# Attention: a unit's transposes directly ahead of the next unit's scores, its value products one turn later

## The chip, the cores and the metric

One core of a Trainium2 chip runs the whole program. The metric is device time in microseconds, the median of repeated executions. TensorE is called PE in what follows, VectorE is DVE, ScalarE is ACT, GpSimd is POOL and SyncE, which issues most loads, is SP.

## What is computed

A diffusion backbone of four layers, over 256 latent tokens (a grid of 4 rows by 64 columns) and 256 context tokens of width 1024. Layers 0 and 3 mix tokens by attention, layer 1 by a convolution module, layer 2 by a gated convolution; after each comes an MLP with squared ReLU. The change touches the two attention layers alone:

```python
q, k, v = split_heads(h_lat @ wqkv, 3)          # 16 heads of 64
q = q * ATTN_SCALE
...
s_lat = jnp.einsum("bhqd,bhaqkd->bhqak", q_r, k_nb)   # window of 16 columns in every grid row
s_lat = s_lat + bias_r
s_ctx = jnp.einsum("bhqd,bhcd->bhqc", q_r, k_c)       # all context keys
p = jax.nn.softmax(concatenate([s_lat, s_ctx]), axis=-1)
...
o = p_lat @ v_nb + p_ctx @ v_c
...
o_lat = o_grid.reshape(b, l, d) @ wo
```

In layer 0 the context tokens are queries too, with a softmax over context keys; in layer 3 only latent tokens are.

## The kernel before

**Units.** Heads are taken in pairs, eight of them. A pair has three units in layer 0 (latent tokens 0 to 127, latent tokens 128 to 255, all context tokens) and the first two of them in layer 3, so there are 24 units and 16. A unit is worked in these steps:

- scores (`attn_scores`, line 714): for both heads a product of 512 columns in three terms, since queries and keys are kept as a high and a low part. One PSUM tile for each head; the pool `mm` has six.
- softmax (`softmax`, lines 729 to 739), for one head after the other: DVE adds bias and mask (729) and takes the negated row maximum (734), ACT takes the exponential (736) with the row sum, DVE its reciprocal (737) and the scaling (739).
- transposes (`attn_transpose`, line 748): PE turns the four blocks of the first head and then of the second through two PSUM tiles of the pool `x`, and ACT copies each tile out (749).
- value products (`attn_out`, line 758): both heads' matmuls alternate. After a pair's last unit `finish` (772, 773) splits the output into high and low part.

**What stands between the steps.** `attn_pairs` is a generator. It yields at fixed places, and `attention` advances it from inside another stream of matmuls: first the query and key projections of the coming pairs (`qks`, one step is six matmuls), later the first half of the output projection (`first_half`, one step is twelve). `interleave` gives six turns of the generator to eight steps of the stream in layer 0 and four to eight in layer 3; beside `first_half` it gives twelve or ten turns to seven steps, so there the pieces stand closer. PE's order is exactly the order in which the code is written here (`manual_schedule`, lines 879 to 896). The other engines' orders come from a scheduler that places their instructions when it builds the program; each engine then works its own list in that order.

**What else is in those lists.** DVE and ACT also split the next pair's weights into high and low part (`split`, lines 223 and 224, two tiles of 128x1024 for each pair), evacuate the projections (820 to 825), update the residual stream (591), and DVE accumulates modulation vectors in the background (lines 314 and 318) from rows that SP loads (line 310). These rows' buffers (tag `mraw`, four of them) are shared with the bias tiles `e` of the softmax: a row is loaded into a buffer once line 729 has read the bias tile there. In layer 0 the background also runs on PE (lines 373 and 382). The transposed probabilities `pt` and the split weights share the tag `w` with ten buffers.

```python
for i in range(len(items) + 1):
    if i < len(items):
        ...
        soft[i] = self.attn_scores(q[hp], k[hp], u, bias[hp])
    yield
    if i > 0:
        ...
            self.attn_transpose(x, u, pt[:, hh])
    yield
    if i > 0:
        weigh(*items[i - 1], pt)
```

Of the kernel before, what the change touches and what calls it, by code (L numbers as in the profile page):

```python
# [8 lines left out]
F32 = mybir.dt.float32  # L9
# [7 lines left out]
P = 128  # L17
D = 1024
KT = D // P
LAT = 256  # L20
# [13 lines left out]
class Net:  # L34
# [726 lines left out]
    def attn_pairs(self, slot, hps, q, k, v, o, units):  # L761

        nc = self.nc
        items = [(hp, u) for hp in hps for u in units]
        bias, soft, pts, out = {}, {}, {}, {}

        def finish(hp):
            ps = out.pop(hp)
            hi, lo = self.hid(F32R), self.hid(F32R)
            n = NTOK if len(units) > 2 else LAT  # L770
            src, a, b = self.turned(ps[:, :n]), self.rows64(hi[:, :n]), self.rows64(lo[:, :n])
            nc.scalar.activation(out=a, in_=src, func=AF.Copy)
            nc.vector.tensor_tensor(out=b, in0=src, in1=a.bitcast(F32), op=ALU.subtract)
            o[hp] = (hi, lo)

        def weigh(hp, u, pt):
            if u == 0:
                out[hp] = self.ps()
            self.attn_out(out[hp], pt, v, hp, u)
            if u == units[-1]:  # L780
                finish(hp)

        for i in range(len(items) + 1):
            if i < len(items):
                hp, u = items[i]
                for p in (hp, hp + 1):
                    if p in hps and p not in bias:
                        bias[p] = [self.bias_tile(slot, 2 * p + hh, q[hp][0] if slot == 0 and hp == 0 else None)
                                   for hh in range(2)]
                soft[i] = self.attn_scores(q[hp], k[hp], u, bias[hp])  # L790
            yield
            if i > 0:
                hp, u = items[i - 1]
                pt = self.wtile([2, 4, P] if u < 2 else [2, 2, LAT], F32)
                for hh, x in enumerate(soft.pop(i - 1)):
                    self.attn_transpose(x, u, pt[:, hh])
            yield
            if i > 0:
                weigh(*items[i - 1], pt)

    def value(self, v, acts, g, tt, i, part, ps):


        if tt not in ps:
            ps[tt] = self.ps()
        s = slice(tt * P, (tt + 1) * P)
        self.mm3(ps[tt], (acts[i][0][:, s], acts[i][1][:, s]), part, i == 0, i == KT - 1)
        if i == KT - 1:
            v[tt, g] = self.work.tile([P, 512], F32, tag=f"u{4 * g + tt}", name=self.name("v"))
            self.nc.scalar.copy(out=v[tt, g], in_=ps[tt])  # L810
# [565 lines left out]
```

## Time and profile before

| what | value |
|---|---|
| median of 3 runs (lowest, highest) | 2176.44 us (2175.43, 2177.57) |
| the profiled execution, its span | 2173.36 us, 2171.5 us |
| PE busy over the span | 2132.5 us (98%) |
| DVE, ACT busy | 1537.9 us (71%), 829.9 us (38%) |
| stretch of attention turns in layer 0 | 104 to 283 us of the span |
| stretch of attention turns in layer 3 | 1844 to 1962 us of the span |

PE is busy nearly throughout, so what counts is where it stands still, and in what these two stretches differ from the rest. A matmul's row in the timeline is longer than its share of the engine, since matmuls overlap: the time that a piece of work takes is read from the start of its first row to the start of the next piece.

### The profile page before, as it was taken

Reading aid. Unit: us, or ns where it says so; the run is one execution under the profiler, and the core shown is the slowest. Engines: PE = TensorE matmul, PEld = TensorE weight load, DVE = VectorE, ACT = ScalarE, POOL = GpSimd, SP = SyncE. Lnnn points to the kernel's source line nnn. Section 1 sums busy time; section 2 is a strip of 40 time slices with the busy share of each in tenths; the row PEclk is TensorE's granted clock in tenths of the full one; section 3 lists DMA queues with packets and bytes.
Section 4 is the critical chain, followed back from the end, with each engine's and each line's share of the span. In section 5 each row is a group of like instructions: output and inputs, shape, how many; then the busy total and the mean of one; then the engine's idle time right before and its main releaser. Section 6 shows DMA issues by size and latency. Waiting matters only on the chain.

```text
span 2171.5 us, 33261 instructions
## 1 busy us (share of the span) xinstructions
PE 2132.5 (98%) x12948; PEld 1782.6 (82%) x12948; DVE 1537.9 (71%) x2727; ACT 829.9 (38%) x1397; POOL 98.5 (5%) x168
## 2 busy tenths in 40 slices
PE   8999999999999999999999999999999999989998
PEld 5777778888889779888888888898888888879998
DVE  5266668986889947978676876597755674778655
ACT  4255534223234226523223332252322333546444
POOL 1122100000000000000000000000000001220000
PEclk9999999999999999999999999999999999999999
DMA  9655544654553551454444444245544535664563
GB/s 302 159 106 118 136 153 153 190 155 154 153 175 112 157 162 50 136 181 152 128 149 148 138 134 145 79 137 175 165 146 140 170 117 131 101 108 155 186 193 107
DMA packets 202188, 318.09 MB, mean 146 GB/s; under 512 B 14669, under 2 KB 67857, under 8 KB 202032
## 3 DMA queue, kind: packets, MB, share of 16 engines
q1 hardware_dynamic: 198080, 309.26, 45.5%
q0 software_dynamic: 3648, 6.61, 4.6%
q8 instruction: 101, 1.65, 0.3%
q14 instruction: 55, 0.45, 0.1%
q10 hardware_dynamic: 304, 0.12, 0.0%
HBM read 313.15 MB, written 2.78 MB: 145 GB/s over the span
## 4 chain that ended last, share of the span: by engine, by line
PE 88%; DVE 4%; ACT 1%; DMA 1%; issue 1%; DVEq 0%; ACTq 0%; SPq 0%
PE mm L106 27%; PE mm L107 26%; PE mm L108 26%; PE mm L1010 2%; PE mm L758 2%; PE mm L714 1%; PE x L748 1%; DVE h L970 1%; DMA mraw<-in_mod_w_dram 1%; DVE w L224 1%; PE mm L373 1%; PE x L492 0%; ACT w L749 0%; PE x L529 0%; DVE t L546 0%
## 5 line engine op out<-in xcount | busy, mean ns | idle before, releaser
L223 ACT ACTIVATE w<-raw 128x1024 fp32r<-128x1024 f32 (+1 forms) x377 | 392.8, 1056 | 683.7 <-PE mm L107 614.3
L106 PE MATMUL mm<-a,w 128*128 128x512 f32 (+2 forms) x1792 | 632.4, 354 | 5.1 <-ACT a L559 4.7
L224 DVE TENSOR_TENSOR w<-raw,w 128x1024 fp32r<-128x1024 f32 (+1 forms) x377 | 452.4, 1219 | 260.8 <-ACT w L223 259.9
L108 PE MATMUL mm<-a,w 128*128 128x512 f32 (+2 forms) x1792 | 624.8, 350 | 4.7 <-DVE w L224 4.7
L107 PE MATMUL mm<-a,w 128*128 128x512 f32 (+2 forms) x1792 | 628.1, 351 | 0.1
L107 PE MATMUL mm<-h,w 128*128 128x256 f32 (+1 forms) x1504 | 505.6, 336 | 0.0
L106 PE MATMUL mm<-h,w 128*128 128x512 f32 (+1 forms) x1376 | 472.2, 344 | 0.0
L108 PE MATMUL mm<-h,w 128*128 128x512 f32 (+1 forms) x1376 | 469.1, 341 | 0.0
L106 PEld LDWEIGHTS mm<-a,w 128*128 128x128 f32 x1792 | 338.6, 189 | 64.0 <-issue 10.2
L108 PEld LDWEIGHTS mm<-a,w 128*128 128x128 f32 x1792 | 339.3, 190 | 52.4 <-DVE w L224 5.9
L107 PEld LDWEIGHTS mm<-a,w 128*128 128x128 f32 x1792 | 339.6, 190 | 45.8 <-DVE a L560 0.8
L318 DVE SCALAR_TENSOR_TENSOR macc<-mraw,cw,macc 128x512 f32<-128x512 f32 x448 | 311.9, 744 | 27.0 <-DMA mraw<-in_mod_w_dram 26.0
L107 PEld LDWEIGHTS mm<-h,w 128*128 128x128 f32 x1504 | 282.8, 188 | 32.0
L106 PEld LDWEIGHTS mm<-h,w 128*128 128x128 f32 x1376 | 258.8, 188 | 37.3 <-issue 2.7
L108 PEld LDWEIGHTS mm<-h,w 128*128 128x128 f32 x1376 | 258.5, 188 | 32.6 <-DVE w L224 0.2
L591 DVE SCALAR_TENSOR_TENSOR x<-mm,mod,x 128x256 f32<-128x256 f32 x288 | 127.5, 477 | 79.5 <-PE mm L108 78.3
L223 ACT ACTIVATE h<-t 128x512 fp32r<-128x512 f32 (+1 forms) x148 | 80.7, 547 | 104.4 <-DVE t L622 90.9
L224 DVE TENSOR_TENSOR h<-t,h 128x512 fp32r<-128x512 f32 (+1 forms) x148 | 86.0, 582 | 25.7 <-ACT h L223 25.4
L622 DVE SCALAR_TENSOR_TENSOR t<-mm,t 128x512 f32<-128x512 f32 (+1 forms) x136 | 78.6, 584 | 35.3 <-ACT t L621 34.8
L621 ACT ACTIVATE t<-mm 128x512 f32<-128x512 f32 (+1 forms) x136 | 69.0, 510 | 89.6 <-PE mm L108 88.7
L736 ACT ACTIVATE t<-mm,s 128x512 f32<-128x512 f32 (+1 forms) x96 | 59.3, 620 | 91.1 <-DVE s L734 83.2
L559 ACT ACTIVATE a<-t,mod 128x256 fp32r<-128x256 f32 x120 | 53.1, 500 | 63.3 <-DVE t L546 63.3
(177 smaller groups left out, 1666.3 us busy)
## 6 DMA issues: line engine op xcount, KB each, us to landing
raw<-in_mlp_w_dram SPq DMA_DIRECT2D x256, 512.0 KB, 4.4
mraw<-in_mod_w_dram SPq DMA_DIRECT2D x288, 256.0 KB, 3.0
raw<-in_na_wqkv_dram SPq DMA_DIRECT2D x64, 256.0 KB, 5.3
raw<-in_mod_w_dram SPq DMA_DIRECT2D x32, 512.0 KB, 4.7
raw<-in_sc_win_dram SPq DMA_DIRECT2D x24, 512.0 KB, 4.4
h<-in_mod_w_dram SPq DMA_DIRECT2D x32, 256.0 KB, 6.5
raw<-in_na_wqkv_dram SPq DMA_DIRECT2D x16, 512.0 KB, 4.7
raw<-in_na_wo_dram SPq DMA_DIRECT2D x16, 512.0 KB, 8.2
```

The costliest lines, as they stand in the source:

```text
L106: mm(out=out, lhsT=a[0], rhs=b[0], start=start, stop=False)
L107: mm(out=out, lhsT=a[0], rhs=b[1], start=False, stop=False)
L108: mm(out=out, lhsT=a[1], rhs=b[0], start=False, stop=stop)
L223: self.nc.scalar.activation(out=hi, in_=src, func=AF.Copy)
L224: self.nc.vector.tensor_tensor(out=lo, in0=src, in1=hi.bitcast(F32), op=ALU.subtract)
L318: nc.vector.scalar_tensor_tensor(out=acc[s], in0=raw, scalar=c, in1=acc[s], op0=ALU.mult, op1=ALU.add)
L559: self.nc.scalar.activation(out=hi[:, c], in_=t, func=AF.Identity, bias=sh)
L591: self.nc.vector.scalar_tensor_tensor(out=x, in0=src[:, o:o + LAT], scalar=self.mod1(layer, m, s, j), in1=x, op0=ALU.mult, op1=ALU.add)
L621: nc.scalar.activation(out=r, in_=src, func=AF.Relu)
L622: nc.vector.scalar_tensor_tensor(out=h, in0=src, scalar=0.0, in1=r, op0=ALU.max, op1=ALU.mult)
L736: nc.scalar.activation(out=soft[:, g], in_=s[:, g], func=AF.Exp, bias=nm[:, i:i + 1], accum_out=sm[:, i:i + 1])
L758: nc.tensor.matmul(out=out[64 * hh:64 * hh + 64, c], lhsT=v[t0 + i, hp // 4][:, f:f + 64], rhs=pt[:, hh, i], start=i == 0, stop=i == n - 1 ...
```

## The change

The loop of `attn_pairs` has two yields a round as before, at other places. Before, a round began with the scores of unit i, and the transposes of unit i-1 came a turn later, its value products another turn later, ahead of the next scores. Now a round begins with the transposes of unit i-1, directly followed by the scores of unit i, and the value products of unit i-1 come one turn later. No instruction is added to PE or taken away.

```diff
--- before.py
+++ after.py
@@ -762,7 +762,7 @@
 
         nc = self.nc
         items = [(hp, u) for hp in hps for u in units]
-        bias, soft, pts, out = {}, {}, {}, {}
+        bias, soft, out = {}, [], {}
 
         def finish(hp):
             ps = out.pop(hp)
@@ -781,22 +781,22 @@
                 finish(hp)
 
         for i in range(len(items) + 1):
+            if i > 0:
+                hp, u = items[i - 1]
+                pt = self.wtile([2, 4, P] if u < 2 else [2, 2, LAT], F32)
+                for hh, x in enumerate(soft.pop()):
+                    self.attn_transpose(x, u, pt[:, hh])
             if i < len(items):
                 hp, u = items[i]
                 for p in (hp, hp + 1):
                     if p in hps and p not in bias:
                         bias[p] = [self.bias_tile(slot, 2 * p + hh, q[hp][0] if slot == 0 and hp == 0 else None)
                                    for hh in range(2)]
-                soft[i] = self.attn_scores(q[hp], k[hp], u, bias[hp])
-            yield
-            if i > 0:
-                hp, u = items[i - 1]
-                pt = self.wtile([2, 4, P] if u < 2 else [2, 2, LAT], F32)
-                for hh, x in enumerate(soft.pop(i - 1)):
-                    self.attn_transpose(x, u, pt[:, hh])
+                soft.append(self.attn_scores(q[hp], k[hp], u, bias[hp]))
             yield
             if i > 0:
                 weigh(*items[i - 1], pt)
+            yield
 
     def value(self, v, acts, g, tt, i, part, ps):
```

On PE, in layer 3 beside the output projection, before: value products (`w_17992` holds turned probabilities), scores of a unit into `mm_18047` and `mm_18048`, and behind them the transposes of the unit before (`t_17963` and `t_17972` are its probabilities).

```order
L758 MATMUL mm_17937<-w_17992,v_16742 64x128 x2
L758 MATMUL mm_17937<-w_17992,v_16747 64x128 x2
L758 MATMUL mm_17937<-w_17992,v_16804 64x128 x2
L758 MATMUL mm_17937<-w_17992,v_16809 64x128 x2
L714 MATMUL mm_18047<-h_17643,h_17544 128x512
L714 MATMUL mm_18048<-h_17643,h_17544 128x512
L714 MATMUL mm_18047<-h_17643,h_17545 128x512
L714 MATMUL mm_18048<-h_17643,h_17545 128x512
L714 MATMUL mm_18047<-h_17644,h_17544 128x512
L714 MATMUL mm_18048<-h_17644,h_17544 128x512
L748 MATMUL x_18074<-ident,t_17963 128x128 x4
L748 MATMUL x_18080<-ident,t_17972 128x128 x4
```

The same place now:

```order
L748 MATMUL x_18048<-ident,t_17976 128x128 x4
L748 MATMUL x_18054<-ident,t_17985 128x128 x4
L714 MATMUL mm_18060<-h_17655,h_17553 128x512
L714 MATMUL mm_18061<-h_17655,h_17553 128x512
L714 MATMUL mm_18060<-h_17655,h_17554 128x512
L714 MATMUL mm_18061<-h_17655,h_17554 128x512
L714 MATMUL mm_18060<-h_17656,h_17553 128x512
L714 MATMUL mm_18061<-h_17656,h_17553 128x512
L758 MATMUL mm_18086<-w_18047,v_16742 64x128 x2
L758 MATMUL mm_18086<-w_18047,v_16747 64x128 x2
L758 MATMUL mm_18086<-w_18047,v_16804 64x128 x2
L758 MATMUL mm_18086<-w_18047,v_16809 64x128 x2
```

The transposes moved ahead of the scores, and the value products of the same unit moved behind them. From a unit's scores to its own transposes there were three turns; now there are two.

On DVE, in layer 3, the softmax of a pair's second unit, before (`mm_` are the scores of the two heads, `macc` the background sum, `mraw` its loaded rows, `w_` and `raw_` the weights that are split):

```order
L729 TENSOR_TENSOR mm_17672<-mm_17672,e_17389 128x256
L729 TENSOR_TENSOR mm_17673<-mm_17673,e_17393 128x256
L734 TENSOR_REDUCE s_17682<-mm_17672 128x1
L737 RECIPROCAL s_17684<-s_17683 128x1
L734 TENSOR_REDUCE s_17691<-mm_17673 128x1
L318 SCALAR_TENSOR_TENSOR macc_17461<-mraw_17647,cw,macc_17461 128x512
L739 TENSOR_SCALAR t_17681<-t_17681,s_17684 128x512
L318 SCALAR_TENSOR_TENSOR macc_17461<-mraw_17650,cw,macc_17461 128x512
L737 RECIPROCAL s_17693<-s_17692 128x1
L821 SCALAR_TENSOR_TENSOR h_17730<-mm_17653,h_17729 128x4x64
L739 TENSOR_SCALAR t_17690<-t_17690,s_17693 128x512
L224 TENSOR_TENSOR w_17735<-raw_17733,w_17734 128x1024
```

The same softmax now:

```order
L729 TENSOR_TENSOR mm_17685<-mm_17685,e_17402 128x256
L729 TENSOR_TENSOR mm_17686<-mm_17686,e_17406 128x256
L734 TENSOR_REDUCE s_17695<-mm_17685 128x1
L224 TENSOR_TENSOR w_17744<-raw_17742,w_17743 128x1024
L224 TENSOR_TENSOR w_17751<-raw_17749,w_17750 128x1024
L318 SCALAR_TENSOR_TENSOR macc_17473<-mraw_17659,cw,macc_17473 128x512
L737 RECIPROCAL s_17697<-s_17696 128x1
L734 TENSOR_REDUCE s_17704<-mm_17686 128x1
L318 SCALAR_TENSOR_TENSOR macc_17473<-mraw_17662,cw,macc_17473 128x512
L739 TENSOR_SCALAR t_17694<-t_17694,s_17697 128x512
L737 RECIPROCAL s_17706<-s_17705 128x1
L821 SCALAR_TENSOR_TENSOR h_17739<-mm_17665,h_17738 128x4x64
L739 TENSOR_SCALAR t_17703<-t_17703,s_17706 128x512
```

The two weight splits (line 224) stood behind the softmax. Now they stand inside it, ahead of the first head's reciprocal (line 737), and the first background product (line 318) moved ahead of it too. Of the sixteen softmaxes of a pair's second unit, nine now hold both splits between lines 734 and 737, and four hold one there and one ahead of line 729; before, none held one there. Three have none, being the last ones beside the output projections.

## Rows read from the trace of the kernel before

**Rows 1.** Busy time by engine in four stretches; columns in the first line.

```profile
core 0: us, PE busy (x) PEld busy (x) DVE busy (x) ACT busy (x) POOL busy (x), PEclk, DMA share, GB/s
104.00:283.00 179.00, 176.39 (x1183) 128.43 (x1182) 110.34 (x250) 94.17 (x218) 34.55 (x50) 1.00 0.51 115
1844.00:1962.40 118.40, 111.86 (x844) 89.78 (x842) 84.09 (x191) 61.36 (x136) 28.69 (x36) 0.97 0.59 96
1905.00:1915.00 10.00, 7.76 (x49) 5.79 (x48) 8.14 (x16) 3.29 (x8) 2.88 (x4) 0.83 0.90 90
1935.00:1945.00 10.00, 7.60 (x50) 5.51 (x48) 9.38 (x21) 3.19 (x8) 3.44 (x5) 0.83 0.73 69
```

**Rows 2.** Timeline of PE, layer 0: start, length, line, operation [idle before].

```profile
124.20 0.95 PE L714 MATMUL mm<-h,h 64*128 64x512 f32 x6
...
126.58 1.03 PE L748 MATMUL x<-ident,t 128*128 128x128 f32 x8
...
128.92 1.79 PE L758 MATMUL mm<-w,v 128*64 128x256 f32 x8
130.64 0.97 PE L714 MATMUL mm<-h,h 64*128 64x512 f32 x6
...
134.42 1.04 PE L748 MATMUL x<-ident,t 128*128 128x128 f32 x8
...
136.77 1.06 PE L373 MATMUL mm<-raw,cw 128*32 128x512 f32 x8
```

**Rows 3.** Timeline of DVE, layer 0: the softmax of the scores of 124.20.

```profile
127.50 0.16 DVE L737 RECIPROCAL s<-s 128x1 f32<-128x1 f32 x1 [0.91 <-ACT t L736]
...
128.16 0.48 DVE L739 TENSOR_SCALAR t<-t,s 128x512 f32<-128x512 f32 x1
...
129.35 0.49 DVE L739 TENSOR_SCALAR t<-t,s 128x512 f32<-128x512 f32 x1
```

**Rows 4.** Timeline of ACT, layer 0: the first exponential of all.

```profile
106.99 1.28 ACT L736 ACT_TABLE_LOAD   x1 [2.59 <-DVE s L734]
```

**Rows 5.** The page's costliest groups: busy us, mean ns, idle before.

```profile
L223 ACT ACTIVATE w<-raw 128x1024 fp32r<-128x1024 f32 (+1 forms) x377 | 392.8, 1056 | 683.7 <-PE mm L107 614.3
```

**Rows 6.** Timeline of PE, layer 3: one unit's scores, transposes, products.

```profile
1864.67 0.96 PE L714 MATMUL mm<-h,h 64*128 64x512 f32 x6
...
1867.10 1.03 PE L748 MATMUL x<-ident,t 128*128 128x128 f32 x8
1867.89 0.37 PE L106 MATMUL mm<-a,w 128*128 128x256 f32 x1
...
1870.18 1.09 PE L758 MATMUL mm<-w,v 128*64 128x128 f32 x16
1871.20 0.96 PE L714 MATMUL mm<-h,h 64*128 64x512 f32 x6
...
1874.99 1.03 PE L748 MATMUL x<-ident,t 128*128 128x128 f32 x8
```

**Rows 7.** Timeline of DVE, layer 3: a softmax with background work in it.

```profile
1898.01 0.67 DVE L734 TENSOR_REDUCE s<-mm 128x1 f32<-128x512 f32 x1
1902.77 0.75 DVE L318 SCALAR_TENSOR_TENSOR macc<-mraw,cw,macc 128x512 f32<-128x512 f32 x1 [4.09 <-DMA mraw<-in_mod_w_dram]
...
1904.89 0.48 DVE L739 TENSOR_SCALAR t<-t,s 128x512 f32<-128x512 f32 x1
1905.28 2.35 DVE L224 TENSOR_TENSOR w<-raw,w 128x1024 fp32r<-128x1024 f32 x2
```

**Rows 8.** Timeline of SP's queue, layer 3: the rows' DMAs issued.

```profile
1896.18 1.38 SPq L310 DMA_DIRECT2D mraw<-in_mod_w_dram  x2
```

**Rows 9.** Timeline of PE, layer 3: a wait and what ran after it.

```profile
1910.30 1.71 PE L758 MATMUL mm<-w,v 128*64 128x128 f32 x16 [2.07 <-ACT w L749]
1911.94 1.65 PE L714 MATMUL mm<-h,h 64*128 64x512 f32 x6
```

## Prediction

> **What bounds the kernel now.** I read the busy time by stretch first. In the two attention stretches PE is busy for 176.4 of 179.0 us and for 111.9 of 118.4 us, so it stands idle for 2.6 and 6.5 us. In two pieces of layer 3 the granted clock averages 0.83 over 10 us: (1-0.83)/0.5 x 10 is 3.4 us at 1.2 GHz instead of 2.4, and half of that, 1.7 us, is lost each time [rows 1]. Then I read PE's timeline and the other engines' beside it. Some waits lie inside a row and count as busy: the products at 128.92 took 1.72 us to the next piece, where others take 1.02 [rows 2, 6]; I put these at about 4 us in all, from that 0.7 us and half a dozen like it. So these stretches lose 2.6 + 6.5 + 3.4 + 4 = 16.5 us now. PE sets the end, and whatever makes it wait there is paid in full.
>
> The reader is to see next how far a unit's softmax is from being late. Scores started at 124.20; their scaled probabilities were there at 128.64 for the first head and 129.84 for the second, 4.4 and 5.6 us later; their transposes started at 134.42, 10.2 us after the scores [rows 2, 3]. Before, 4.6 us of slack lay there, and softmax time cost nothing.
>
> **The change part by part.** No matmul is added, and the moved steps issue no DMA. Three things change.
>
> First, the distance. I build it from starts in the rows: scores and 6 matmuls of 512 columns 2.4 us, scores and 12 of them 3.8, 6 alone 1.5 (2.34 from transposes to products, less 0.8 for the transposes), a mod matmul group 1.0 [rows 2]; products 1.0, transposes 0.8, in layer 3 scores and 12 matmuls of 256 columns 2.4, and 12 mixed ones 2.3 [rows 6]. Two turns now hold, from scores to transposes:
> layer 0, first unit of a pair 2.4 + 1.0 + 1.5 = 4.9 us, second unit 3.8 + 1.0 + 1.5 = 6.3, third 2.4 + 1.0 + 2.9 = 6.3, each 1.0 more where a mod matmul falls in;
> layer 3, first unit 3.8 + 1.0 + 2.3 = 7.1, second 2.4 + 1.0 + 2.3 = 5.7;
> beside the output projections 4.8 to 5.9 in layer 0 and 3.5, 3.5, 5.0, 3.5, 5.0 in layer 3 for its last five units.
> The second head's transposes begin 0.4 us later (half of 0.8), so a unit waits by what its second head's 5.6 us exceed this distance plus 0.4, at the least.
>
> Second, the softmax itself gets longer in 13 units, since weight splits now stand inside it. Two splits take 2.35 us on DVE [rows 7]; the reciprocal behind them waited 0.91 us for the exponential anyway [rows 3], so they add about 1.5: 7.2 us for the second head instead of 5.6. On ACT two splits of 1.06 us stand ahead of the exponential [rows 5]; they run while the scores do, and I add nothing for them. In five units of layer 3 two background products of 0.75 us stand in the softmax too. One of them waited 4.09 us for its rows, which were issued at 1896.18 and were there at 1902.77, after 6.6 us [rows 7, 8]. Now the splits' 2.35 us run during that wait, and weight loads no longer go out just ahead of it. The wait of such a softmax is bounded by 0 and by 4.1; I take 0 and add 0.9 to 1.0 for the products, so 8.1 us.
>
> The sum of what PE waits after the change:
> - the very first unit has a table load of 1.28 us in its softmax [rows 4]; its probabilities come 6.1 and 7.1 us after the scores, its transposes 3.8: 2.9 us. It is the same in layer 3 with more cover: 1.0.
> - layer 0, a first unit without a mod matmul, 5.6 - 5.3, once: 0.3. Second units without one, 7.2 - 6.7, twice: 1.0. Third units: 0.
> - layer 0 beside the output projection, five units with 6.1 to 7.5 us of softmax (splits in one, updates of the residual in the others) against 4.8 to 5.9: 1.2 + 0.9 + 1.2 + 0.8 + 0.4 = 4.5.
> - layer 3, second units with splits: one without background 7.2 - 6.1, less 0.2 of cover by ACT, 0.9; three with it 2.0 each (8.1 - 6.1); the first of all, whose splits come in two places, 2.2: 9.1.
> - layer 3, the last five: 8.4 - 3.9, then 6.1 - 3.9, 5.9 - 5.4, 5.9 - 3.9 and 6.0 - 5.4: 4.5 + 2.2 + 0.5 + 2.0 + 0.6 = 9.8.
> - where scores and products follow the transposes at once, the products wait some 0.25 us for ACT's copies, five times: 1.3.
> That is 2.9 + 1.0 + 0.3 + 1.0 + 4.5 + 9.1 + 9.8 + 1.3 = 29.9 us. Two slow stretches of the clock stay, as before; half of that time the softmax runs on meanwhile, so 1.7. In all 31.6.
>
> Third, what goes: all of the 16.5. Its largest piece, 2.07 us of products waiting for copies behind a late softmax [rows 9], and its companions turn into the waits above.
>
> The new neighbours on PE, scores right behind transposes, do not occur in the trace. Scores behind products run at once with 0.96 us, and a matmul behind transposes starts its successor 0.1 late [rows 6]. So 40 such places cost between -2.4 and +2.4 us; I take 0.
>
> 31.6 - 16.5 = +15 us. The profiled execution took 2173.4 us, with 2171.5 of span and 1.9 around it; it comes to 2188.4. The median of the runs is 3 us above that execution, so I forecast 2176.4 + 15 = **2191 us**, with 2183 to 2199 as this case's own range.
>
> When a transpose waits, PE holds behind it the next scores and the whole stream of projections; DVE and ACT then catch up, so one late softmax does not delay the next.
>
> **The rivals.**
> *The clock falls more often.* In the trace the granted clock fell to 1.2 GHz after the wait of 2.07 us ended at 1910.30: the products there took 1.64 us to the scores' start, against 1.02 [rows 6, 9]. After the change eight waits have 2 us or more, not two. If each brings the clock down for what such a stretch lost, it is 6 x 1.7 = 10 us more, less a few that a slower PE gives the softmax back: 2199. The waits between 1 and 1.4 us that I see in the trace were mostly not followed by it, which speaks against it. The Trainium skill (TensorE: Matmul & The Clock Gate, HAM oscillation) says that pauses between bursts of matmuls bring the clock down again and again, so that each burst starts slow; the trace shows it for two pauses of this length and leaves open whether the new ones are of the kind. By that rule this case would be the one to come.
>
> *No difference.* The waits that go and those that come are of one size, if the splits inside the softmax cost nothing (their 1.5 us in 13 units, of which about 6 us stand in the sum) and the last five units wait half as long: 31.6 - 6 - 5 = 20.6 against 16.5, within 4 us of 2176.4. For it speaks that DVE is busy for only 84 of 118 us in layer 3 [rows 1]. Against it, that these spare times lie elsewhere than between scores and transposes.
>
> *Faster.* The splits now run half a pair ahead of their use, and so do the loads that wait for their buffers; DVE had kept the second unit's softmax 4.09 us for loaded rows, behind which the splits came at 1905.28, and the products waited at 1910.30 [rows 7, 9]. If that chain was the whole loss of layer 3 and is gone, 6.5 + 3.4 + 2 come back there, and the new waits are those that no order avoids: 2.9 + 1.0 in the two first units and 0.3 + 1.7 + 1.7 + 0.2 + 1.7 + 0.2 for a 5.6 us softmax, 9.7 in all. 16.5 - 9.7 gives 2169.6. It decides from the point where a second unit's softmax in layer 3 takes less than 6.1 us, the distance plus 0.4. Against it: the order of DVE puts 2.35 us of splits into just this softmax.
>
> **How the numbers follow.** Forecast 0.50, clock 0.18, no difference 0.16, faster 0.16. A measurement of this kernel can tell about 0.2%, 4.4 us, from no change. Forecast and clock are both slower; at the forecast's low end a little falls to no difference, and the case of no difference is wide enough to reach both sides: slower 0.68, same 0.18, faster 0.14. The range must hold 0.8: below, it takes in the case of no difference and a part of the faster one, to 2172; above, the clock's 2199 and a row wait of 4 us in two softmaxes, to 2206.
>
> **What would show it.** In the profile afterwards: transposes (line 748) with waits for line 739 in the second units of layer 3, about 2 us each, and the largest, 4 to 5 us, in the unit whose products follow the next unit's scores at once beside layer 3's output projection; no products waiting 2 us for copies; the first unit's transposes 2 to 3 us late around 108 us. PE idle in the layer 3 stretch about 18 us instead of 6.5, in the layer 0 stretch about 8 instead of 2.6. The loaded rows' wait at line 318 is to be short. I am wrong if the second units' transposes come without a wait, or if the layers between the two stretches change their time.

## The result, and the profile after

The changed kernel takes 2191.13 us (median of 4 runs, 2190.3 to 2193.07), the kernel before 2175.93 us beside it: a ratio of 1.0068, with an interval of 1.0056 to 1.0080. It is slower by 15.2 us. Its profiled execution has a span of 2188.7 us, 17.2 more than that of before.

Where the time went can be read without any model, since the 11,764 PE instructions that are not scores, transposes or value products stand in the same order in both kernels. Their starts, after less before, differ by 0.4 us where layer 0's units begin, by 7.7 where they end (283.06 against 290.72), by 7.9 at the first scores of layer 3 (1844.34 against 1852.21) and by 17.2 behind its units (2014.41 against 2031.65). So layer 0 costs 7.3 us, layer 3 costs 9.4, and the 1561 us of program between the two 0.2.

The busy time of the engines in the two stretches and in three pieces of them, after the change (columns as in [rows 1], to which they answer):

```profile
104.00:291.00 187.00, 181.44 (x1188) 128.97 (x1187) 112.09 (x254) 98.99 (x220) 29.95 (x52) 0.99 0.52 115
1852.00:1979.10 127.10, 112.08 (x831) 87.15 (x829) 85.72 (x188) 65.01 (x136) 29.35 (x36) 0.99 0.45 90
108.00:118.00 10.00, 6.86 (x29) 4.49 (x27) 6.86 (x14) 7.39 (x14) 2.43 (x4) 0.83 0.43 117
1910.00:1920.00 10.00, 8.61 (x62) 6.64 (x61) 7.89 (x16) 4.73 (x10) 2.83 (x4) 1.00 0.80 176
1945.00:1955.00 10.00, 6.45 (x42) 5.04 (x43) 7.00 (x14) 3.22 (x8) 2.88 (x4) 0.83 0.86 190
```

PE is idle for 5.6 us in layer 0 (2.6 before) and for 15.0 in layer 3 (6.5 before). The clock is low in two pieces of 10 us again, one of which has moved from layer 3 to layer 0.

PE's timeline in layer 3 shows a round of the new order, with a pair's second unit in it (it answers to [rows 6]; the projections between are left out but for one):

```profile
1907.78 1.04 PE L748 MATMUL x<-ident,t 128*128 128x128 f32 x8
1908.75 0.96 PE L714 MATMUL mm<-h,h 64*128 64x512 f32 x6
1909.64 0.39 PE L106 MATMUL mm<-a,w 128*128 128x256 f32 x1
...
1911.26 1.09 PE L758 MATMUL mm<-w,v 128*64 128x128 f32 x16
...
1915.90 0.63 PE L748 MATMUL x<-ident,t 128*128 128x128 f32 x4 [1.23 <-DVE s L737]
1916.68 0.63 PE L748 MATMUL x<-ident,t 128*128 128x128 f32 x4 [0.16 <-DVE t L739]
1917.24 0.95 PE L714 MATMUL mm<-h,h 64*128 64x512 f32 x6
```

Two things are to be seen. The scores of 1908.75 have their transposes at 1915.90, which stand idle first and stop again between the two heads: 1.4 us and 0.3 more than a round without a wait takes. And the transposes at 1907.78, which wait for nothing, need 0.97 us until the next piece starts, where transposes ahead of a projection took 0.79 (1867.10 to 1867.89, [rows 6]).

DVE's timeline of the same softmax (it answers to [rows 7]):

```profile
1909.75 0.76 DVE L729 TENSOR_TENSOR mm<-mm,e 128x256 f32<-128x256 f32 x2 [1.15 <-PE mm L714]
1910.42 0.68 DVE L734 TENSOR_REDUCE s<-mm 128x1 f32<-128x512 f32 x1
1911.02 2.35 DVE L224 TENSOR_TENSOR w<-raw,w 128x1024 fp32r<-128x1024 f32 x2
1913.28 0.75 DVE L318 SCALAR_TENSOR_TENSOR macc<-mraw,cw,macc 128x512 f32<-128x512 f32 x1
...
1916.06 0.48 DVE L739 TENSOR_SCALAR t<-t,s 128x512 f32<-128x512 f32 x1
```

The second head is there at 1916.54, 7.8 us after the scores began. Both splits stand in it, and the background product behind them (line 318) no longer waits for its rows: in layer 3 these waits went from 8.9 us, four of them, to 0.8 us.

The first unit of all and the largest wait, on PE (the first answers to the table load of [rows 4]):

```profile
104.54 0.97 PE L714 MATMUL mm<-h,h 64*128 64x512 f32 x6
...
111.08 0.66 PE L748 MATMUL x<-ident,t 128*128 128x128 f32 x4 [2.60 <-DVE t L739]
112.27 0.66 PE L748 MATMUL x<-ident,t 128*128 128x128 f32 x4 [0.54 <-DVE t L739]
112.85 1.48 PE L714 MATMUL mm<-h,h 64*128 64x512 f32 x6
...
1942.56 0.96 PE L714 MATMUL mm<-h,h 64*128 64x512 f32 x6
1943.45 1.09 PE L758 MATMUL mm<-w,v 128*64 128x128 f32 x16
...
1949.71 1.94 PE L748 MATMUL x<-ident,t 128*128 128x128 f32 x8 [3.55 <-DVE s L737]
```

The first unit's transposes come 2.8 us late and lose 0.7 between the heads. In layer 3 the products follow the scores at once, one step of the output projection is all the cover, and 4.4 us are lost: 3.6 to 3.7 of waiting, and the rest because the transposes themselves already run at the slow clock (1.94 us instead of 1.04). The clock is slow right after each of these two waits, and nowhere else in the two stretches: the scores at 112.85 take 1.42 us to the next piece instead of 0.89.

The loads changed too. First, before (1844 to 1962 us), the queues of POOL (q0) and SP (q1) in layer 3: packets, MB, share of the time of the 16 DMA engines; and the issues by tile: engine, operation and count, KB each, median us from issue to landing. Then the issues after (1852 to 1979 us).

```profile
q0 software_dynamic: 1152, 2.36, 36.6%
q1 hardware_dynamic: 7840, 8.91, 22.7%
...
raw<-in_na_wo_dram SPq DMA_DIRECT2D x8, 512.0 KB, 10.8
mraw<-in_mod_w_dram SPq DMA_DIRECT2D x10, 256.0 KB, 4.9
```

```profile
raw<-in_na_wo_dram SPq DMA_DIRECT2D x8, 512.0 KB, 4.1
mraw<-in_mod_w_dram SPq DMA_DIRECT2D x10, 256.0 KB, 2.9
```

The same weights land in less than half the time, and the rows in 2.9 us instead of 4.9. When they are issued shows on the queues of SP and POOL, around one pair before (weights by SP, bias tiles by POOL):

```profile
1904.07 2.81 POOL L687 DMA_DIRECT2D e<-in_na_rpb_dram  x4 [3.27 <-DVE t L739]
...
1906.53 1.51 SPq L95 DMA_DIRECT2D raw<-in_na_wo_dram  x2
```

and around one pair after:

```profile
1912.26 1.51 SPq L95 DMA_DIRECT2D raw<-in_na_wo_dram  x2
...
1914.58 2.83 POOL L687 DMA_DIRECT2D e<-in_na_rpb_dram  x4 [7.00 <-DVE s L737]
```

Before, the weights were asked for while the bias tiles were under way; now they go 2.3 us ahead of them, because the splits free their buffers inside the softmax. The bias tiles cost the DMA engines much for their size: before, POOL's 1152 packets took 36.6% of the 16 engines' 118 us, 0.60 us each on the mean, and SP's 7840 packets 22.7%, 0.055 us each; after the change the same packets take 21.9% and 22.3%. The Trainium skill (DMA: Bandwidth & Descriptors, Queues, rings and completion order) says that a DMA engine takes one packet from a queue and then one from the next; by that rule a load beside the bias tiles waits for one of their long packets between two of its own, and these rows agree with it.

**The sum.** For each step from one PE instruction to the next I took what it is longer than the shortest of its kind, in the two stretches. Before, these excesses are 6.1 us in layer 0 and 11.1 in layer 3; after, 8.9 and 19.0, so the waits grew by 10.7 us (the slow clock's part is in them). To this come 33 rounds that are dearer by 0.2 us each without any wait, most of it in the 0.97 us just seen (e3, e10 and e11 below show what it is), 6.6 us. Together 17.3, against the 17.2 that the two executions differ by.

### The profile page after: what moved, and what is told of

It reads as the page before. It is cut to its first block, busy times and chain, and to the rows that moved or that the text cites. A ratio compares the mean times of both kernels' runs of the same rounds, so it can differ in the third digit from the quotient of the medians.

```text
span 2188.7 us, 33283 instructions
## 1 busy us (share of the span) xinstructions
PE 2138.1 (98%) x12948; PEld 1781.1 (81%) x12948; DVE 1538.1 (70%) x2727; ACT 836.7 (38%) x1397; POOL 95.2 (4%) x168
```

## The experiments

Two of my theories changed on the way, so they stand nearly in the order in which they ran (e12 and e13 were the last). All kernels are timed against the kernel before, run beside them. "PE waits" are the excesses just described; the last two columns are layer 3's, from its first scores to its last products.

| run | median us | ratio to before (interval) | PE waits, layer 0 / 3 | weights to landing | waits for rows |
|---|---|---|---|---|---|
| before | 2175.5 to 2176.8 | 1 | 6.1 / 11.1 | 10.8 | 8.9 |
| the change | 2191.13 | 1.0068 (1.0056, 1.0080) | 8.9 / 19.0 | 4.1 | 0.8 |
| e1, layer 0 only | 2183.22 | 1.0033 (1.0021, 1.0046) | 7.8 / 12.7 | 11.0 | 11.3 |
| e2, layer 3 only | 2185.94 | 1.0051 (1.0039, 1.0064) | 6.4 / 19.4 | 4.4 | 0.9 |
| e3, scores first | 2183.25 | 1.0032 (1.0019, 1.0044) | 8.8 / 11.8 | 10.5 | 6.3 |
| e4, splits behind | 2194.06 | 1.0082 (1.0069, 1.0096) | 11.2 / 19.1 | 10.6 | 3.8 |
| e5, products between | 2223.84 | 1.0229 (1.0209, 1.0248) | 24 / 39 | 3.5 | 1.3 |
| e6, five turns | 2180.28 | 1.0023 (1.0014, 1.0033) | 9.2 / 9.2 | 10.7 | 7.9 |
| e7, four turns | 2171.75 | 0.9988 (0.9979, 0.9997) | 4.8 / 2.7 | 4.2 | 0.7 |
| e8, five turns, more cover | 2175.34 | 1.0000 (0.9991, 1.0008) | 4.7 / 10.9 | 11.0 | 8.9 |
| e12, a row buffer more | 2182.06 | 1.0026 (1.0017, 1.0035) | 5.6 / 11.9 | 8.0 | 9.4 |
| e13, that and splits behind | 2205.19 | 1.0133 (1.0119, 1.0148) | 9.9 / 19.0 | 7.4 | 8.2 |
| e10, four turns in layer 3 | 2167.00 | 0.9956 (0.9943, 0.9970) | 6.2 / 3.0 | 4.2 | 1.1 |
| e11, three switches in layer 3 | 2166.05 | 0.9951 (0.9939, 0.9964) | 6.3 / 2.8 | 3.7 | 0.6 |

**One layer alone (e1, e2).** The new place of the transposes holds for one layer; the other keeps the old one.

```diff
-            if i > 0:
+            if slot == 0 and i > 0:       # e2: slot == 1
                 ...                        # transposes ahead of the scores
             yield
+            if slot != 0:
+                ...                        # transposes here, and a turn
+                yield
```

> The new order in layer 0 only; layer 3 keeps the old one. Theory (the loss is local to each stretch: late softmaxes behind two turns instead of three, and a dearer step from transposes to scores): the stretch of layer 0 took 7.4 us more in the changed kernel's trace than before, so 2175.9 + 7 = 2183 us (2181 to 2185). Rival (the loss sits where the second units of layer 3 wait, layer 0 costs nothing that a measurement sees, as its softmaxes are seldom late): 2176 to 2179 us.

> The new order in layer 3 only; layer 0 keeps the old one. Theory: the stretch of layer 3 took 9 us more in the changed kernel's trace, so 2175.9 + 9 = 2185 us (2183 to 2187), and the excess over before of this run and that of layer 0 alone add up to the 15.2 us of the whole change. Rival (the parts do not add, since the order in layer 0 also shifts what the background work finds in layer 3): the two sum to less than 12 or more than 19 us.

Measured: 7.0 and 9.8 us over before. The parts add up to 16.8, with 15.2 for the whole, which the intervals allow, and each lies where the traces put it. The loss is local to the stretches.

**Scores ahead of transposes (e3).**

```diff
-            ...    # transposes of unit i-1, then scores of unit i
+            ...    # scores of unit i, then transposes of unit i-1
             yield
             ...    # products of unit i-1
             yield
```

> As the change, but a unit's scores directly ahead of the transposes of the unit before, instead of behind them. The turns from scores to transposes stay two; 0.9 us of scores now stand in that distance, and no scores follow transposes. Theory (PE steps from transposes to scores 0.18 us dearer in 38 places, 6.6 us, and each late transpose waits on the distance): the 6.6 us go, each wait falls by up to 0.9 us, about 10 us over some 14 waits, some of it given back by value products that wait for the copies beside the output projections: 2191 - 6.6 - 9 = 2175 us (2171 to 2179). Rival 1 (the order of these two costs nothing by itself, only the waits count): 2182 us. Rival 2 (the waits come from the splits on VectorE alone, whatever stands between): 2184 us or more.

Measured: 2183.25 us, 8 us less than the change but 8 more than the theory said; nearest to rival 1. The trace shows why in a part without any wait:

```profile
1871.64 0.97 PE L714 MATMUL mm<-h,h 64*128 64x512 f32 x6
1872.54 1.09 PE L748 MATMUL x<-ident,t 128*128 128x128 f32 x8
...
1878.32 0.97 PE L714 MATMUL mm<-h,h 64*128 64x512 f32 x6
```

A first unit's round takes 6.68 us here (1871.64 to 1878.32), with transposes that lead straight into projections; in the change's order, where nothing waits, 6.72 (1864.71 to 1871.43 in e10), and before 6.53 (1864.67 to 1871.20, [rows 6]). So it is not the pair "transposes, then scores" that is dear: the round is dearer by 0.15 to 0.2 us in either order. What the change and e3 share is that scores and products stand apart, each with projections or transposes on both sides; before, products led into scores. And in layer 3 only one split stands between lines 734 and 737 of a softmax, instead of eleven in the change; weights take 10.5 us, and the rows kept DVE waiting for 3.97 us at 1924.02, so part of before's loss in layer 3 came back.

**Splits behind the softmax (e4).** The split's DVE half is kept in program order, for the weights that are loaded in the attention stretches.

```diff
+        low = self.nc.vector.tensor_tensor(out=lo, in0=src, in1=hi.bitcast(F32), op=ALU.subtract)
+        keep and self.tc.keep_in_program_order(low)
...
-                        ahead = self.weights(w, 0, KT, segs(hp + 1))
+                        ahead = self.weights(w, 0, KT, segs(hp + 1), keep=True)
```

> As the change, but the weight splits of the attention stretches are kept in program order on VectorE, so that they stand behind a softmax, as before the change, and no longer inside it. Theory (two splits inside lengthen a softmax by about 1.5 us, which PE pays where the softmax is late already): the waits of the second units of layer 3, 9.0 us in the changed kernel's trace, fall to 2 to 3, those of layer 0's by about 1: 2191 - 7 = 2184 us (2182 to 2187). Rival (the splits run in time in which the softmax waits for the exponential anyway, so the shorter distance alone makes the waits): 2190 to 2192 us.

Measured: 2194.06 us, 3 us more than the change, though the two intervals overlap. Theory and rival both miss. The theory is right where nothing else comes in: the waits of four second units in layer 3 fall from 1.9, 0.7, 1.4 and 1.7 us to 1.0, 0, 0.8 and 0.9. So two splits inside cost 0.7 to 0.9 us of wait, not 1.5. But the weights now meet the bias tiles again, and one softmax waits for rows as before the change. DVE, then PE behind it:

```profile
1915.72 0.75 DVE L318 SCALAR_TENSOR_TENSOR macc<-mraw,cw,macc 128x512 f32<-128x512 f32 x1 [2.70 <-DMA mraw<-in_mod_w_dram]
```

```profile
1917.02 0.63 PE L748 MATMUL x<-ident,t 128*128 128x128 f32 x4 [2.10 <-DVE t L739]
1918.47 1.08 PE L748 MATMUL x<-ident,t 128*128 128x128 f32 x4 [0.82 <-DVE t L739]
```

That one unit loses 3.7 us (1.7 in the change), part of it to the slow clock, in which its second head already runs (1.08 us instead of 0.63); in layer 0 the splits now delay two third units by 0.9 us each. The splits inside the softmax are not the fault of the change: they cost and give back about the same.

**Products between transposes and scores (e5).** Products one round later, so that a round is transposes, products, scores, and then two turns.

```diff
-            ...    # transposes of unit i-1
-            ...    # scores of unit i
-            yield
-            ...    # products of unit i-1
-            yield
+            ...    # transposes of unit i-1
+            ...    # products of unit i-2
+            ...    # scores of unit i
+            yield
+            yield
```

> As the change (transposes of unit i-1, then scores of unit i, two turns a round), with the value products of unit i-2 between the two, so that products lead into scores as before the change. The distance from scores to transposes is the change's. Theory after the first four runs: what PE pays for the new order beside its waits, 0.17 us a unit, is not a matter of which of scores and transposes comes first but of how often a round switches between pieces of full 128x128 tiles (projections, transposes) and pieces of 64 rows or 64 columns (scores, products): three times before, four times in the change and in the run with scores first, three times here. So the waits stay as in the change and about 6.6 us go: 2191 - 6.6 = 2184.5 us (2181 to 2187; fewer splits stand inside a softmax here, 11 instead of 22, which pulls downwards). Rival (transposes at the side of scores cost by the change of tile, however many there are; or the trace's 0.17 us is modelled only): 2190 to 2192 us.

Measured: 2223.84 us, far from theory and rival. I had called the distance unchanged, but the products had stood between scores and transposes, and now they don't: 1.0 us less. PE in layer 0, where the change had hardly a wait:

```profile
186.76 0.97 PE L714 MATMUL mm<-h,h 64*128 64x512 f32 x6
...
192.01 0.63 PE L748 MATMUL x<-ident,t 128*128 128x128 f32 x4
193.21 0.63 PE L748 MATMUL x<-ident,t 128*128 128x128 f32 x4 [0.57 <-DVE t L739]
```

The transposes of 29 of the 40 units are late now (17 in the change), and the waits grow by 35 us over the change's. Some 29 us of that stand at the transposes, 1.0 us for each late unit; most of the rest is the slow clock, whose mean over layer 3's stretch is 0.92 here and 0.99 in the change. As a measurement of the distance this is the sharpest of all: after two turns most units stand at the edge, and a microsecond less costs a microsecond in each of those; most third units of layer 0 still wait for nothing. On the switches it says nothing.

**Five turns, old neighbours (e6, e8).** Scores one unit further ahead in the old order; e8 also gives n + 8 turns instead of n + 6 to the first half of the output projection.

```diff
-        for i in range(len(items) + 1):
+        for i in range(len(items) + 2):
...
-                for hh, x in enumerate(soft.pop(i - 1)):
+                for hh, x in enumerate(soft.pop(i - 2)):
...
-                weigh(*items[i - 1], pt)
+                weigh(*items[i - 2], pt)
```

> The old order with scores taken one unit further ahead: scores of unit i, a turn, transposes of unit i-2, a turn, products of unit i-2. Five turns lie between scores and transposes instead of three, three switches a round as before. Theory (the distance decides: the old order loses about 15 us to late softmaxes in two stretches, and with two turns more none is late but at the very end, where one to three turns run without cover): 2176 - 15 + 3 = 2164 us (2160 to 2169). Rival 1 (the losses come from what DVE has to do, the rows' wait of 4 us or the splits, and are only moved to another unit by more distance): 2172 to 2177 us. Rival 2 (longer life of probabilities blocks buffers): 2178 us or more.

> As the run with five turns, and beside the first half of the output projection two turns more for its seven steps (14 instead of 12 in layer 0, 12 instead of 10 in layer 3), so that the last turns have cover. Theory (with five turns the only waits left are at the end of each stretch): 1 to 3 us faster than without, 2162 us (2158 to 2168). Rival (turns that stand closer there make softmaxes late earlier, as the last five units of layer 3 show in the change): the same or up to 3 us slower.

Measured: 2180.28 and 2175.34 us, so the theory falls: distance alone does not take the old order's loss away. By its time e6 lies in rival 2's range and e8 in the one that rival 1 had for e6; the trace of e6 shows something of both. DVE:

```profile
1905.50 0.75 DVE L318 SCALAR_TENSOR_TENSOR macc<-mraw,cw,macc 128x512 f32<-128x512 f32 x1 [2.87 <-DMA mraw<-in_mod_w_dram]
...
1908.01 2.36 DVE L224 TENSOR_TENSOR w<-raw,w 128x1024 fp32r<-128x1024 f32 x2
```

ACT and PE:

```profile
1912.06 0.69 ACT L736 ACTIVATE t<-mm,s 128x512 f32<-128x512 f32 x1 [6.11 <-DVE s L734]
...
1912.74 1.06 ACT L749 COPY w<-x 128x512 f32<-128x512 f32 x2
```

```profile
1908.94 1.04 PE L748 MATMUL x<-ident,t 128*128 128x128 f32 x8
...
1913.36 1.57 PE L758 MATMUL mm<-w,v 128*64 128x128 f32 x16 [1.30 <-ACT w L749]
```

The transposes run in time at 1908.94. Their copies, though, stand on ACT behind the next softmax's exponential, and that waits until DVE has got over the rows and the splits. So the products wait, as for the 2.07 us of [rows 9]: this part of the old order's loss comes through ACT's list, where no distance between scores and transposes helps. It is not all of it: of the 6.5 us that PE stood idle in layer 3 before, 3.3 are transposes that wait for line 739 itself (1936.43, 1938.13, 1946.16), and those are gone in e6. In their place stands e6's largest wait in layer 3, which is rival 2's kind:

```profile
1943.04 1.65 PE L714 MATMUL mm<-h,h 64*128 64x512 f32 x5 [1.67 <-DVE h L773]
```

Scores of the second head stop until line 773 has read a pair's output, it seems for the PSUM tile that this frees, and line 773 stands on DVE behind late rows (1.20 us) and two splits. The cover of e8 brought 5 us, more than either side expected.

**Four turns, joined as in the change (e7).**

```diff
-        for i in range(len(items) + 1):
-            if i > 0:
-                hp, u = items[i - 1]
+        for i in range(len(items) + 2):
+            if i > 1:
+                hp, u = items[i - 2]
...
-                weigh(*items[i - 1], pt)
+                weigh(*items[i - 2], pt)
```

> The change with one unit more between: transposes of unit i-2 directly ahead of the scores of unit i, products of unit i-2 a turn later. Four turns lie between scores and transposes instead of two; everything else of the change, its four switches a round too, stays. Theory (of the change's loss 28.9 us are waits that two more turns take away, while its dearer steps, 6.6 us, stay): the time of the run with five turns and the old order, plus 6.6 us, so 2170.5 us (2166 to 2176), and in the trace transposes of 0.97 us ahead of scores throughout. Rival 1 (the steps cost nothing, only the waits do): the same time as the run with five turns, within 2 us. Rival 2 (distance does not matter): 2190 us.

Measured: 2171.75 us, where the theory had 2170.5; the comparison with e6 fell, since that run was not what I took it for. Against the change only the distance differs, and 19 us go. The waits are 4.8 and 2.7 us, and the transposes take 0.97 us throughout: before's 17.2 us less 7.5, and 6.6 more for the steps, is 3 us faster than before, as measured (3.7).

**A buffer more for rows (e12, e13).** Five buffers instead of four for the tag `mraw`, in the old order and in e4 (the other two lines that use the tag change alike).

```diff
-                raw = self.work.tile([P, 512], F32, tag="mraw", bufs=4, name=self.name("mraw"))
+                raw = self.work.tile([P, 512], F32, tag="mraw", bufs=5, name=self.name("mraw"))
```

> The kernel before with five buffers instead of four for the background's rows and the bias tiles. Theory (what the old order loses in layer 3, 11 us in its trace, starts at one place each time: a background product in a second unit's softmax waits 2.7 to 4.1 us for rows whose buffer came free late, the splits follow, and ACT's copies stand behind the next exponential): with one buffer more the rows are asked for earlier, VectorE's waits for rows at line 318 in layer 3 fall below 1 us, and most of the 11 us go: 2175.5 - 8 = 2167 us (2163 to 2172). Rival (rows take as long as they take, and the wait comes back at another unit, since one more buffer changes only which softmax holds the product): 2174 to 2178 us.

> The change with the weight splits kept behind the softmax (the run with splits behind took 2194 us, where VectorE waited 2.7, 0.4 and 0.3 us for rows inside three softmaxes and the clock fell three times), and with five buffers for rows and bias tiles. Theory (splits and late rows take each other's place: splits inside hide the rows' wait, without them it shows, and only without both does a softmax come back to its bare length): the second units of layer 3 wait 2 to 3 us in all instead of 8.7 in the change, so about 2184.5 us (2181 to 2188). Rival (the distance alone sets these waits, a softmax is as late without splits and late rows): 2189 us or more.

Measured: 2182.06 and 2205.19 us, both slower than without. In e12, DVE twice waits over 3 us again:

```profile
1898.56 1.01 DVE L318 SCALAR_TENSOR_TENSOR macc<-mraw,cw,macc 128x512 f32<-128x512 f32 x1 [3.27 <-DMA mraw<-in_mod_w_dram]
...
1925.40 1.05 DVE L318 SCALAR_TENSOR_TENSOR macc<-mraw,cw,macc 128x512 f32<-128x512 f32 x1 [3.36 <-DMA mraw<-in_mod_w_dram]
```

These rows had been issued 7.8 and 5.9 us before (at 1890.76 and 1919.47), so it is not the late buffer alone that makes rows late; the rival's mechanism holds, though the time lies above its range. The buffer also shifted loads elsewhere: e12's profiled execution is 5.9 us longer, and 6.7 us stood already ahead of layer 0's units. The two runs say little on the softmax and nothing on the distance.

**A version that beats both (e10, e11).** Layer 0 in the old order. In layer 3, e10 is e7; e11 makes a round of transposes, products and scores, and then two turns, with distance enough.

```diff
+            ...    # layer 3, e11: transposes of unit i-2
+            ...    # products of unit i-3
+            ...    # scores of unit i
+            yield
+            yield
```

> Layer 0 in the old order; in layer 3 transposes of unit i-2 directly ahead of the scores of unit i, products a turn later (the run with four turns, in layer 3 alone). Theory (in the run with four turns layer 0 cost 4.9 us against before, the four switches a round and a longer first wait, while layer 3 gained 8.2): 2175.5 - 8 = 2167.5 us (2165 to 2171). Rival (the gain in layer 3 hangs on the state that layer 0 leaves, as buffers and the background's progress): 2171 to 2175 us.

> Layer 0 in the old order; in layer 3 one piece a round of transposes of unit i-2, products of unit i-3 and scores of unit i, then two turns of projections. About as far from scores to transposes as the run before this one, so no late softmax, but three switches between full and split tiles a round instead of four. Theory (0.17 us a switch, 15 units): 2.6 us less than the run with four turns in layer 3 alone, 2165 us (2161 to 2169), with transposes that lead into products in 0.97 us and products into scores in 1.02. Rival 1 (switches cost nothing in time): the same as that run, within 1 us. Rival 2 (turned probabilities that live a round longer keep weight buffers): 3 us or more slower than that run, with projections that wait for splits.

Measured: 2167.00 and 2166.05 us, 0.44% and 0.49% faster than before, e10 as expected. Here no softmax is late for most of layer 3, and the price of the steps stands alone. PE in e10, one pair from transposes to transposes, and then in e11, one pair from scores to scores:

```profile
1856.65 1.03 PE L748 MATMUL x<-ident,t 128*128 128x128 f32 x8
1857.62 0.97 PE L714 MATMUL mm<-h,h 64*128 64x512 f32 x6
...
1871.43 1.03 PE L748 MATMUL x<-ident,t 128*128 128x128 f32 x8
```

```profile
1863.69 1.09 PE L758 MATMUL mm<-w,v 128*64 128x128 f32 x16
1864.72 0.97 PE L714 MATMUL mm<-h,h 64*128 64x512 f32 x6
...
1879.10 0.96 PE L714 MATMUL mm<-h,h 64*128 64x512 f32 x6
```

The same matmuls take 14.78 us in e10 and 14.38 in e11; before they took 14.40 (scores of 1864.67 to scores of 1879.07). A round that changes the kind of tile four times (full, 64 rows, 64 columns) is dearer by 0.2 us than one with three changes, whatever the order in it: that is shown, row by row. The medians, 1.0 us apart where 2.6 were expected, would not have told theory and rival 1 apart: one unit of e11 waits 2.1 us beside the output projection.

## Why the prediction came out, and where it was wrong

The time forecast and the time measured are both 2191 us. By its own steps:

- **Distance, two turns instead of three.** Right, and the cause of the waits: e7 takes them away with distance alone, e5 makes them of 1.0 us less. Waits of the second units of layer 3: forecast 9.1 us, measured 7.5. The last five there: 9.8 forecast and measured, the largest 4.4 where 4.5 stood, though some 0.8 us of the measured sum is the slow clock in that largest one. The first unit of layer 0: 2.9 forecast, 3.5 measured; in layer 3 1.0 and 1.1. Other units of layer 0 ahead of the output projection 1.3 and 1.3, beside it 4.5 forecast, 2.5 measured. Products that wait for copies: 1.3 forecast, 0.2 measured. PE's idle time was forecast as 18 and 8 us, and is 15.0 and 5.6.
- **Splits inside the softmax, 1.5 us each.** Half of it: 0.7 to 0.9 (e4). What I had not seen is their other side, that they send the next weights off ahead of the bias tiles; without them (e4) the run was no faster.
- **The rows' wait at line 318, bounded by 0 and 4.1 us, taken as 0.** Right (0.8 us in all of layer 3), for the reason given, that the splits run in that time, and for one more: the rows land in 2.9 us instead of 4.9.
- **What goes, 16.5 us.** 17.2 by the step-by-step sum.
- **New neighbours on PE, between -2.4 and +2.4 us, taken as 0.** This step failed: 6.6 us, outside its own bounds. The prediction looked at pairs of neighbours by the length of their rows, 0.96 us for scores, instead of at how often a round changes the kind of tile, three times before and four now.
- **The clock, 1.7 us for two slow stretches.** Two stretches, as said. The scores in them lost 0.5 and 0.6 us, the projections at 114.27 1.0 more, the transposes at 1949.71 some 0.8. One of its readings was wrong: the products at 1910.30 before were for the most part not slow. The granted clock is 1.00 until 1911.6 there; their 1.64 us hold a second wait, for the other head's copy, and the slow part begins with the scores at 1911.94 (1.58 us to the next piece).

So the waits were forecast too high (31.6, with the clock, against 27.9) and the steps too low by 6.6; in the traces the sum was 15 against 17.2. The medians differ by 15.2, and there it fits. That the number was met to the microsecond is luck; that the change is slower, and by late softmaxes above all, is not.

Of the rivals, *the clock falls more often* did not come, since its eight waits of 2 us or more did not: only two units waited so long, 3.5 and 3.7 us, and behind both the clock fell. Three second units of layer 3 wait 1.5 to 1.7 us, and the granted clock there is 1.00 (1910 to 1920 in the first fence shows one). The Trainium skill's rule (TensorE: Matmul & The Clock Gate, HAM oscillation), that pauses bring the clock down, held in the changed kernel for the longest pauses alone. The length of one pause does not decide it: before, the second slow stretch (1938.9 to 1942.3) came not behind a pause of 2 us, as the prediction has it, but behind two of half that,

```profile
1936.43 0.63 PE L748 MATMUL x<-ident,t 128*128 128x128 f32 x4 [1.04 <-DVE t L739]
1938.13 0.63 PE L748 MATMUL x<-ident,t 128*128 128x128 f32 x4 [1.07 <-DVE t L739]
```

and in e11 a wait of 1.9 us (1932.28) left the clock at 1.00. What decides stays open. *Faster* was half right: the chain of rows, splits, exponential and copies went away as it said. But the second unit's softmax took 7.8 us in the round shown and not under 6.1, and e7, e10 and e11 show that its gain can be had with two turns more. *No difference* fails on the last five units, which wait as long as forecast.

Left open: that loads beside the bias tiles are what makes the rows late is read from landing times in fourteen kernels (weights in 3.5 to 4.4 us and 0.6 to 1.3 us of waits for rows where six to eleven of layer 3's splits stand inside the softmaxes, 7.4 to 11.0 us and 3.8 to 11.3 us where none or one does). No run moved a load alone.

## What to carry to other kernels

Measure the slack of a producer before taking a turn from it, and count in it every piece that stands between, the moved one too: here two turns left most units at the edge, where 4.6 us of slack had stood in layer 0, and the next microsecond cost 33 us. Count also how often a round changes the kind of matmul tile (full, 64 rows, 64 columns), and keep pieces of 64 rows and of 64 columns side by side. An early instruction on a busy engine may be worth its delay by what it lets start: look at the transfers that it releases, and at what they then run beside.

## What the hardware did unexpectedly

A change of the kind of tile (full 128x128, 64 rows, 64 columns) shows as a step of 0.20 us from the last matmul of one kind to the first of the other (transposes to scores, products to scores, products to projections), where a projection follows the last transpose after 0.03 us. Products and then scores side by side have one such step between them, and save the second. And loads of 512 KB, issued the same way, took 4.1 us (median) where they went ahead of the bias tiles' loads and 10.8 where they went behind them.
